# A bias table with fewer copies, PSUM reads moved between engines, and input sums formed in place, in a decoder layer

## The chip, the cores and the metric

The kernel runs on one core of a Trainium2 chip. The metric is the time of one execution on the device in microseconds (us). Engines are named as the profile names them: PE is TensorE's matmul stream, PEld its weight loads, DVE is VectorE, ACT is ScalarE, POOL is GpSimd and SP is SyncE, whose queue (SPq) issues every DMA of this kernel.

## The reference, cut to what matters

One decoder layer on 512 tokens of width 1024 in float32: a SwiGLU feed-forward (FFN) of width 2816, two token mixers side by side (sparse attention with a relative bias, and a gated linear recurrence), their merge, a second such FFN, and a gated per-layer embedding. The two parts that the change touches:

```python
def swiglu(x, w_gate, w_up, w_down):
    return (jax.nn.silu(x @ w_gate) * (x @ w_up)) @ w_down

dist = jnp.maximum(t_pos[None, :, None] - idx, 0)
bias = jnp.moveaxis(rel_bias[rel_bucket(dist)], -1, 2)          # 32 buckets, 8 heads
logits = (jnp.einsum('bqhc,bqkc->bqhk', ql, c_sel) * ATT_SCALE + bias)
```

## The kernel before, in words

**Matmuls.** Every float32 product is three passes: weights and inputs are split into a high part (`hi`, ScalarE copy) and a low part (`lo`, VectorE subtract), and the passes are hi x hi, lo x hi and hi x lo. All of them are issued by one helper, so nearly every row of PE has line L248. A 128x1024 piece of weights arrives in a `raw` tile (5 buffers), and its hi and lo go into a `w` tile (6 buffers of 2112 elements per partition, of which 2048 are used, from an offset `shift`: 0 for plain weights, `SHIFT` for paired ones).

**An FFN** works on 22 column tiles of gate and up in four groups of 6, 4, 6 and 6 tiles. After each group its part of the down product is added to `y`. In the first group four tiles are computed plainly (512 tokens at a time) and two as a pair; all other tiles go in pairs, so an FFN has 1 + 2 + 3 + 3 = 9 pairs.

**A pair** (`pair`, L492) computes two gate tiles (side i = 0) and two up tiles (side i = 1) by Strassen-Winograd's seven half-size products in place of eight. A side needs four sums of weight halves: S1 (POOL, L513), S2 (DVE, L514), S3 (POOL, L517) and S4 (DVE, L520), in place in `raw` or in a sum tile `s` (2 buffers), each then split by ACT (L489) and DVE (L490). The seven products run in the order of `SEVEN`; each is 12 matmuls of 256 columns for each side, so a pair has 7 x 2 x 12 = 168 matmuls. Bank a takes the products number 0, 2, 4 and 6 on top of one another and is read after each: product 6 can't begin on a side before the bank was read for number 4, where C22 = a + P5 is formed (L542, DVE, out of PSUM). POOL then scales side 0's half by R (L551).

**The input sums** (`input_sums`, L459) make T1 to T4 from halves of the scaled input `h`, for all pairs of an FFN, in four steps (k = 0 to 3), each with two scaled copies (`b1`, `b2`: ACT, L467), four POOL subtractions (L471) and four splits (L195, L196). Results of the subtractions go into an `s` tile of the pair's own two buffers. One step is taken before the plain tiles that come next, one after each of them, and what is left ahead of the first pair. `b1`, `b2` and all temporaries of the plain tiles (`hidden`, L372: three each) and of the pairs (four each) are `t` tiles, of which there are 6.

**The bias table** (`bias_vector`, L143) is made at the end of FFN 1's first group: a small matmul and one DVE instruction give `bv` (8 heads on 8 partitions, 384 values each), and one DMA (L157) writes it to DRAM as `bias_d`, 128 copies for each head. Attention later reads it back once for each head (L701) as a 128x256 tile `tp`, in which partition p holds the vector from element 127 - p on: in `bias_d` that is one access pattern, with a step of 383 elements from a partition to the next, which moves to the next copy and one element back.

**Order of the work.** The order on each engine is chosen when the program is built, by a scheduler that follows the order of the code and its own estimate of times; each engine, and the SP queue, then takes its instructions strictly in that order. An instruction that waits holds up all that stand behind it on its engine.

Of the kernel before, what the change touches and what calls it, by code (L numbers as in the profile page):

```python
# [7 lines left out]
F32 = mybir.dt.float32  # L8
# [3 lines left out]
OP = mybir.AluOpType  # L12
PSUM = bass.MemoryType.PSUM

P = 128
# [11 lines left out]
SEVEN = (("a", True, "A11", "B11"), ("b", True, "A12", "B21"), ("a", False, "S2", "T2"), ("c", True, "S1", "T1"),  # L27
         ("a", False, "S3", "T3"), ("c", False, "S4", "B22"), ("a", False, "A22", "T4"))

SHIFT = 16  # L30
FULL = slice(0, NT)
HALF = (slice(0, 256), slice(256, NT))
G_OFF = {n: 8 * i for i, n in enumerate(
# [5 lines left out]
HEADS = 8  # L39
# [11 lines left out]
LEVELS = (1, 2, 4, 8, 16)  # L51
NEAR = 256
BVEC = 384
LEAD = 1
BANKS = {"mm": 2, "pl": 2, "hg": 2, "pt": 1, "po": 1}

# [22 lines left out]
class Layer:  # L79
    def __init__(self, ctx, tc, a, out):  # L80
        self.tc, self.nc, self.a, self.out = tc, tc.nc, a, out

        def pool(name, **kw):
            return ctx.enter_context(tc.tile_pool(name=name, bufs=1, **kw))

        self.const = pool("const")
        self.keep = pool("keep")
        self.wpool = pool("wpool")
        self.tmp = pool("tmp")
        self.psum = pool("psum", space=PSUM)  # L90
        self.dram = pool("dram", space=bass.MemoryType.DRAM)
        self.h_d = self.dram.tile([KT, P, NT], F32, name="h_d")
        self.gate_d = self.dram.tile([2 * KT, P, NT], F32, name="gate_d")
        self.proj_d = self.dram.tile([4, P, D], F32, name="proj_d")
        self.bias_d = self.dram.tile([HEADS, P, BVEC], F32, name="bias_d")
        self.ahead = []
        self.mixing = False
        self.first = {k: iter(v) for k, v in FIRST.items()}
        self.ring = itertools.cycle(("mm", "pl", "mm", "pl", "pt", "po"))
        self.held = None  # L100
        self.lo_engine = self.nc.vector
        self.consts()
# [40 lines left out]
    def bias_vector(self):  # L143


        nc, c = self.nc, self.const
        onehot = self.t(BVEC)[:32]
        nc.sync.dma_start(onehot, self.a["onehot"])
        rel = c.tile([32, HEADS], F32, name="rel")
        nc.sync.dma_start(rel, self.a["rel_bias"])  # L150
        far = c.tile([HEADS, 1], F32, name="far")
        nc.sync.dma_start(far, self.a["rel_far"])
        ps = self.bank("pl")
        nc.tensor.matmul(ps[:HEADS, :BVEC], rel, onehot, start=True, stop=True)
        bv = self.t(BVEC)[:HEADS]
        nc.vector.tensor_scalar(bv, ps[:HEADS, :BVEC], far, 1.0 / ATT_SCALE, op0=OP.subtract, op1=OP.mult)
        nc.sync.dma_start(self.bias_d, bv.unsqueeze(1).to_broadcast([HEADS, P, BVEC]))  # L157

    def gain(self, n):
        return self.vecs[:, G_OFF[n]:G_OFF[n] + KT]  # L160
# [220 lines left out]
    def ffn(self, name, nxt, y, pool, spill=None, begin=None):  # L381
        nc, a = self.nc, self.a
        wg, wu, wd = (a[f"{name}_w_{s}"] for s in ("gate", "up", "down"))
        post = self.ghalf[f"{name}_post"]
        hid_hi = pool.tile([P, INNER, NT], F32R, name="hid_hi")
        hid_lo = pool.tile([P, INNER, NT], F32R, name="hid_lo")
        acc = self.accum(NT)
        for f0, nf, plain in GROUPS:
            first, last = f0 == 0, f0 + nf == FT
            j0 = 0  # L390
            if first and not begin:
                j0 = 2
                w = [self.first_weights(name, (wg[j], wu[j]), D) for j in range(j0)]
                for cols, tags in zip(HALF, (("mm", "mm", "pl", "pl"), ("pt", "po", "mm", "mm"))):
                    ps = [[self.bank(t)[:, :256] for t in tags[2 * j:2 * j + 2]] for j in range(j0)]
                    self.mm3s([(ps[j][i], w[j][i]) for j in range(j0) for i in range(2)], self.hg_hi, self.hg_lo, KT, cols)
                    for j in range(j0):
                        self.hidden(hid_hi, hid_lo, j, *ps[j], cols)
            elif first:
                j0 = 1  # L400
                w = begin[0](wg[0], wu[0])
                ps = self.bank("pl"), self.bank("pt")
                self.mm3s(list(zip(ps, w)), self.hg_hi, self.hg_lo, KT, FULL)
                begin[1]()
                self.hidden(hid_hi, hid_lo, 0, *ps, FULL)
            if first:
                sums = self.input_sums(f"{name}_pre", pool)
                next(sums)
            for j in range(j0, plain):
                pg, pu = self.bank(), self.bank()  # L410
                self.mm3(pg, self.weight(wg[f0 + j], D), self.hg_hi, self.hg_lo, KT, FULL)
                self.mm3(pu, self.weight(wu[f0 + j], D), self.hg_hi, self.hg_lo, KT, FULL)
                self.hidden(hid_hi, hid_lo, j, pg, pu, FULL)
                next(sums, None)
            if first:
                for _ in sums:
                    pass
            for j in range(plain, nf, 2):
                self.pair(pool, [src[f0 + j:f0 + j + 2] for src in (wg, wu)], hid_hi, hid_lo, j)
            w = {}  # L420

            def parts(m, ps, cols, ks):
                if m not in w:
                    w[m] = self.weight(wd[m][:, f0 * P:(f0 + nf) * P], nf * P)
                for k in ks:
                    self.mm3_step(k, ps, w[m], hid_hi, hid_lo, nf, cols)

            def store(m, ps, cols):
                if first:
                    nc.scalar.copy(y[:, m, cols], ps)  # L430
                else:
                    nc.vector.tensor_tensor(y[:, m, cols], y[:, m, cols], ps, op=OP.add)
                if last:
                    self.square_sum(acc[:, cols], y[:, m, cols], m == 0, nc.vector if m == KT - 1 else nc.gpsimd)

            def product(m, cols):
                ps = self.bank()[:, :cols.stop - cols.start]
                parts(m, ps, cols, range(nf))
                store(m, ps, cols)


            early = 3
            ps = [self.bank() for _ in range(early)]
            for ks in (range(nf - 2), range(nf - 2, nf)):
                for m in range(early):
                    parts(m, ps[m], FULL, ks)
            for m in range(early):
                store(m, ps[m], FULL)
            if last:
                self.last_product(product, y, acc, post, nxt, TURN[name], spill, early)  # L450
                if begin:
                    self.ple_proj(pool)
            else:
                for m in range(early, KT):
                    product(m, FULL)
                if first and begin:
                    begin[2]()

    def input_sums(self, gname, pool):  # L459

        nc = self.nc
        self.T = [pool.tile([P, 2, 4, 256], F32R, tag="T", name=f"T{i}", bufs=4) for i in range(4)]
        one, two = HALF
        for k in range(4):
            b1, b2 = self.t(), self.t()
            for b, kk in ((b1, k), (b2, k + 4)):
                nc.scalar.activation(b, self.h[:, kk, :], AF.Copy, scale=self.gain(gname)[:, kk:kk + 1])  # L467
            s = self.sum_tile(pool).rearrange("p (i t) -> p i t", i=4)
            for i, (x, z) in enumerate(((b1[:, two], b1[:, one]), (b2[:, two], s[:, 0]), (b2[:, two], b1[:, two]),
                                        (b2[:, one], s[:, 1]))):  # L470
                nc.gpsimd.tensor_tensor(s[:, i], x, z, op=OP.subtract)  # L471
                self.split(self.T[i][:, 0, k, :], self.T[i][:, 1, k, :], s[:, i])
            yield

    def sum_tile(self, pool):
# [16 lines left out]
    def pair(self, pool, srcs, hid_hi, hid_lo, j):  # L492


        nc = self.nc
        pool_, dve = nc.gpsimd, nc.vector
        low, high = slice(0, 512), slice(512, 1024)
        one, two = HALF
        sides = []
        last = self.weight_tile(SHIFT)  # L500
        for i, src in enumerate(srcs):
            r = [self.raw_tile() for _ in range(2)]
            for x, z in zip(r, src):
                nc.sync.dma_start(x, z)
            w = [self.weight_tile(SHIFT) for _ in range(3)]
            s = self.sum_tile(pool)
            at = {"A11": (w[0], low), "A12": (w[0], high), "S1": (w[1], low), "S2": (w[1], high), "S3": (w[2], low),
                  "A22": (w[2], high), "S4": (last, (low, high)[i])}
# [22 lines left out]
        def after(i, n):  # L531
# [7 lines left out]
            elif n == 3:  # L539
                keep(i, "P5", "c", "acc")  # L540
            elif n == 4:
                dve.tensor_tensor(o2[:, two], b["a"], k["P5"], op=OP.add)  # L542
            elif n == 5:
                dve.tensor_tensor(o1[:, two], b["c"], k["U2"], op=OP.add)
                if i == 0:
# [144 lines left out]
    def attention(self, hd):  # L690


        nc = self.nc
        o, m = hd % 2, hd // 2
        rows = slice(o * IDX, (o + 1) * IDX)
        if o == 0:
# [1 line left out]
        kh = self.kh[o]  # L698
        st = self.stacked(self.qa[m], o, 0)
        tp = self.mixp.tile([P, NEAR], F32, tag="tp", name="tp", bufs=2)  # L700
        nc.sync.dma_start(tp, bass.AP(tensor=self.bias_d.tensor, offset=self.bias_d.offset + hd * P * BVEC + P - 1,  # L701
                                      ap=[[BVEC - 1, P], [1, NEAR]]))
        po = self.bank("po")
        pair = slice(m * P, (m + 1) * P)
        yield
# [550 lines left out]
```

## Time and profile before

| | |
|---|---|
| median of 3 runs | 1279.94 us (1278.24 to 1281.02) |
| profiled execution | 1276.73 us |
| its span, first to last instruction | 1274.9 us |
| busy share PE, DVE, ACT, POOL | 94%, 73%, 51%, 43% |
| mean granted TensorE clock | 0.983 |

The profiled execution stands 3.2 us under the median and 1.8 us over its own span. Times in the rows are counted from the first instruction. A busy share is of the whole span; matmuls overlap, so PE's is an upper bound of its work. In a row of a timeline the bracket gives how long the engine sat idle before the instruction, and which instruction ended that wait.

### The profile page before, as it was taken

The numbers are of one execution on the slowest core, as the hardware profiler recorded it, in microseconds if no ns is written. First come the engines' busy times: TensorE is split into PE (matmuls) and PEld (weight loads), VectorE is DVE, ScalarE is ACT, GpSimd is POOL, SyncE is SP. The second block draws the span as 40 slices with busy tenths as digits, with TensorE's granted clock in tenths as the row PEclk, the third lists the DMA queues.
The fourth block names the chain that finished last, engine by engine and source line by source line (L and its number), as shares of the span: only waits on it lengthen the run. The fifth ranks groups of instructions, "written<-read, shape, count | busy, mean of one in ns | idle before, by whom it ended". The sixth has DMA issues, their size and how long they took to land.

```text
span 1274.9 us, 19983 instructions
## 1 busy us (share of the span) xinstructions
PE 1196.0 (94%) x7532; PEld 1068.4 (84%) x7532; DVE 926.4 (73%) x1532; ACT 644.9 (51%) x1155; POOL 547.8 (43%) x524
## 2 busy tenths in 40 slices
PE   7999299999999999999899999999799999999997
PEld 6888298989999887887688878898689899899976
DVE  7774278976967749999657658477757788678586
ACT  6553143534545546555667655455545444355353
POOL 3532133433446304453747552444433344344474
PEclk9999599999999999999999999999899999999999
DMA  8042332241354412322222226320222323233231
GB/s 277 3 154 58 67 110 98 88 144 67 110 189 158 149 50 67 116 92 80 86 88 92 79 80 219 123 84 29 75 96 71 128 92 124 83 101 117 98 117 66
DMA packets 47897, 131.52 MB, mean 103 GB/s; under 512 B 5400, under 2 KB 10680, under 8 KB 47800
## 3 DMA queue, kind: packets, MB, share of 16 engines
q1 hardware_dynamic: 47800, 130.24, 31.9%
q8 instruction: 59, 0.97, 0.3%
q14 instruction: 38, 0.31, 0.1%
HBM read 118.16 MB, written 12.06 MB: 102 GB/s over the span
## 4 chain that ended last, share of the span: by engine, by line
PE 55%; DVE 25%; issue 8%; ACT 5%; POOL 4%; DMA 3%; SPq 0%; DVEq 0%; POOLq 0%; ACTq 0%
PE mm L248 21%; PE pl L248 15%; PE pt L248 6%; PE po L248 6%; DVE w L490 5%; DVE w L174 2%; DVE hg_lo L293 2%; DVE sc L687 2%; DVE h L347 2%; DVE z L345 1%; DVE small L686 1%; DMA g<-gate_d 1%; PE po L736 1%; DVE s L514 1%; DMA raw<-ffn_w_gate 1%
## 5 line engine op out<-in xcount | busy, mean ns | idle before, releaser
L248 PE MATMUL mm<-hg_hi,w 128*128 128x512 f32 (+1 forms) x984 | 268.1, 355 | 3.4 <-ACT hg_hi L195 1.5
L248 PEld LDWEIGHTS mm<-hg_hi,w 128*128 128x128 f32 x984 | 170.9, 189 | 27.3 <-ACT hg_hi L195 1.7
L172 ACT ACTIVATE w<-raw 128x1024 fp32r<-128x1024 f32 (+5 forms) x149 | 135.1, 913 | 87.2 <-PE mm L248 24.4
L174 DVE TENSOR_TENSOR w<-raw,w 128x1024 fp32r<-128x1024 f32 (+5 forms) x133 | 146.9, 1112 | 38.2 <-ACT w L172 37.7
L248 PE MATMUL mm<-hg_lo,w 128*128 128x512 f32 (+1 forms) x492 | 172.9, 353 | 1.3 <-DVE hg_lo L293 1.3
L490 DVE TENSOR_TENSOR w<-raw,w 128x1024 fp32r<-128x1024 f32 (+1 forms) x108 | 146.1, 1368 | 19.3 <-ACT w L489 19.3
L513 POOL TENSOR_TENSOR s<-raw 128x512 f32<-128x512 f32 x36 | 52.5, 1459 | 220.2 <-DMA raw<-ffn_w_gate 110.2
L248 PE MATMUL pl<-hg_hi,w 128*128 128x256 f32 (+1 forms) x504 | 111.7, 314 | 27.6 <-ACT acc L529 22.5
L489 ACT ACTIVATE w<-raw 128x1024 fp32r<-128x1024 f32 (+1 forms) x108 | 95.6, 912 | 61.1 <-DMA raw<-ffn_w_up 26.1
L248 PEld LDWEIGHTS pl<-hg_hi,w 128*128 128x128 f32 x504 | 82.8, 193 | 32.9 <-ACT acc L529 22.7
L248 PEld LDWEIGHTS mm<-hg_lo,w 128*128 128x128 f32 x492 | 92.2, 188 | 13.2 <-DVE hg_lo L293 1.5
L286 POOL TENSOR_TENSOR acc<-acc,sq 128x256 f32<-128x256 f32 x78 | 67.5, 870 | 58.9 <-ACT sq L285 54.8
L248 PE MATMUL mm<-T,w 128*128 128x256 f32 x552 | 74.2, 284 | 7.7 <-DVE t L542 4.3
L248 PE MATMUL pl<-hid_hi,w 128*128 128x512 f32 (+1 forms) x276 | 78.2, 367 | 0.0
L248 PE MATMUL pl<-hg_lo,w 128*128 128x256 f32 (+1 forms) x252 | 77.6, 311 | 0.7 <-DVE hg_lo L293 0.7
L514 DVE TENSOR_TENSOR s<-s,raw 128x512 f32<-128x512 f32 x36 | 32.3, 896 | 63.1 <-POOL s L513 63.1
L248 PEld LDWEIGHTS mm<-T,w 128*128 128x128 f32 x552 | 68.8, 192 | 9.2 <-DVE t L542 5.1
L489 ACT ACTIVATE w<-s 128x1024 fp32r<-128x1024 f32 x36 | 38.2, 1062 | 75.3 <-DVE s L514 23.7
L248 PE MATMUL pl<-T,w 128*128 128x256 f32 x540 | 72.3, 283 | 3.9 <-ACT w L489 2.0
L248 PE MATMUL mm<-hid_hi,w 128*128 128x512 f32 (+1 forms) x264 | 73.9, 365 | 0.0
L248 PEld LDWEIGHTS pl<-T,w 128*128 128x128 f32 x540 | 67.4, 192 | 4.9 <-ACT w L489 2.2
L578 POOL TENSOR_TENSOR t<-t,R 128x512 f32<-128x512 f32 x36 | 59.2, 1647 | 25.9 <-ACT t L577 25.8
(358 smaller groups left out, 3026.5 us busy)
## 6 DMA issues: line engine op xcount, KB each, us to landing
raw<-ffn_w_gate SPq DMA_DIRECT2D x43, 512.0 KB, 4.0
raw<-ffn_w_up SPq DMA_DIRECT2D x43, 512.0 KB, 3.6
raw<-ffn_w_down SPq DMA_DIRECT2D x48, 384.0 KB, 3.8
raw<-w_gates SPq DMA_DIRECT2D x16, 512.0 KB, 3.5
raw<-ffn_w_down SPq DMA_DIRECT2D x16, 256.0 KB, 2.7
gate_d<-t SPq DMA_DIRECT2D x16, 256.0 KB, 2.0
raw<-w_br SPq DMA_DIRECT2D x8, 512.0 KB, 3.5
raw<-w_out SPq DMA_DIRECT2D x8, 512.0 KB, 3.9
```

What stands on the lines that cost most here:

```text
L172: hi = nc.scalar.activation(w[:, 0, c], raw[:, c], AF.Copy)
L174: lo = eng.tensor_tensor(w[:, 1, c], raw[:, c], w[:, 0, c].bitcast(F32), op=OP.subtract)
L248: i = self.nc.tensor.matmul(*args, **kw)
L286: eng.tensor_tensor(acc[:, c:c + 256], acc[:, c:c + 256], sq, op=OP.add)
L293: lo = nc.vector.scalar_tensor_tensor(self.hg_lo[:, k, cols], self.h[:, k, cols], g, self.hg_hi[:, k, cols].bitcast(F32), op0=OP.mult, op1 ...
L347: eng.tensor_tensor(self.h[:, k, c], self.h[:, k, c], z, op=OP.add)
L489: self.nc.scalar.activation(w[:, 0], raw, AF.Copy)
L490: eng.tensor_tensor(w[:, 1], raw, w[:, 0].bitcast(F32), op=OP.subtract)
L513: pool_.tensor_tensor(s[:, low], r[1][:, low], r[1][:, high], op=OP.add)
L514: dve.tensor_tensor(s[:, high], s[:, low], r[0][:, low], op=OP.subtract)
L578: nc.gpsimd.tensor_tensor(z, z, self.R, op=OP.mult)
L687: nc.vector.match_replace(sc, best, sc, TAKEN)
```

## The change

There are five edits:

- `bias_d` holds 23 copies for each head in place of 128. The read for attention steps by (376, 16 times) and (383, 8 times): partition 8a + b reads copy a + b from element 127 - 8a - b on, which are the same values as before.
- C22: ACT copies the PSUM bank into `o2`, then POOL adds P5 to it in SBUF. One DVE instruction less and one more on ACT and on POOL, for each side of each pair.
- The input sums go into a `t` tile and, for T3 and T4, into halves of `b1` and `b2` themselves, not into an `s` tile.
- Two steps of the input sums, not one, are taken before the plain tiles.
- The offset of paired weights in their `w` tile goes in turn through 16, 8, 20 and 12 elements from pair to pair, where it was always 16.

```diff
-SHIFT = 16
+SHIFT = (16, 8, 20, 12)
+STEP = 8
+COPIES = P // STEP + STEP - 1
...
-        self.bias_d = self.dram.tile([HEADS, P, BVEC], F32, name="bias_d")
+        self.bias_d = self.dram.tile([HEADS, COPIES, BVEC], F32, name="bias_d")
+        self.shift = itertools.cycle(SHIFT)
...
-        nc.sync.dma_start(self.bias_d, bv.unsqueeze(1).to_broadcast([HEADS, P, BVEC]))
+        nc.sync.dma_start(self.bias_d, bv.unsqueeze(1).to_broadcast([HEADS, COPIES, BVEC]))
...
                 sums = self.input_sums(f"{name}_pre", pool)
                 next(sums)
+                next(sums)
...
-            s = self.sum_tile(pool).rearrange("p (i t) -> p i t", i=4)
-            for i, (x, z) in enumerate(((b1[:, two], b1[:, one]), (b2[:, two], s[:, 0]), (b2[:, two], b1[:, two]),
-                                        (b2[:, one], s[:, 1]))):
-                nc.gpsimd.tensor_tensor(s[:, i], x, z, op=OP.subtract)
-                self.split(self.T[i][:, 0, k, :], self.T[i][:, 1, k, :], s[:, i])
+            s = self.t()
+            for i, (o, x, z) in enumerate(((s[:, one], b1[:, two], b1[:, one]), (s[:, two], b2[:, two], s[:, one]),
+                                           (b1[:, two], b2[:, two], b1[:, two]), (b2[:, one], b2[:, one], s[:, two]))):
+                nc.gpsimd.tensor_tensor(o, x, z, op=OP.subtract)
+                self.split(self.T[i][:, 0, k, :], self.T[i][:, 1, k, :], o)
...
-        last = self.weight_tile(SHIFT)
+        shift = next(self.shift)
+        last = self.weight_tile(shift)
...
-            w = [self.weight_tile(SHIFT) for _ in range(3)]
+            w = [self.weight_tile(shift) for _ in range(3)]
...
             elif n == 4:
-                dve.tensor_tensor(o2[:, two], b["a"], k["P5"], op=OP.add)
+                nc.scalar.copy(o2[:, two], b["a"])
+                pool_.tensor_tensor(o2[:, two], o2[:, two], k["P5"], op=OP.add)
...
-        nc.sync.dma_start(tp, bass.AP(tensor=self.bias_d.tensor, offset=self.bias_d.offset + hd * P * BVEC + P - 1,
-                                      ap=[[BVEC - 1, P], [1, NEAR]]))
+        nc.sync.dma_start(tp, bass.AP(tensor=self.bias_d.tensor, offset=self.bias_d.offset + hd * COPIES * BVEC + P - 1,
+                                      ap=[[BVEC - STEP, P // STEP], [BVEC - 1, STEP], [1, NEAR]]))
```

## Rows read from the trace of the kernel before

**Rows 1.** The page: granted TensorE clock in 40 slices, in tenths
```profile
PEclk9999599999999999999999999999899999999999
```

**Rows 2.** Waits of PE: for which instruction, us in total, times, longest
```profile
PE pl L248 <- ACT acc L529: 22.5, 1, 22.5
...
PE mm L248 <- DVE t L542: 4.3, 4, 2.1
...
PE pl L248 <- DVE t L542: 1.0, 1, 1.0
```

**Rows 3.** Timeline around the bias table's DMA: SP queue, ACT, PE (start, duration)
```profile
114.30 0.79 SPq L157 DMA_DIRECT2D bias_d<-t  x1
115.76 14.31 SPq L504 DMA_DIRECT2D raw<-ffn_w_up  x2
...
149.93 1.06 ACT L489 ACTIVATE w<-raw 128x1024 fp32r<-128x1024 f32 x1 [26.15 <-DMA raw<-ffn_w_up]
...
151.29 0.80 PE L248 MATMUL pl<-hg_hi,w 128*128 128x256 f32 x2 [22.49 <-ACT acc L529]
...
155.78 2.93 PE L248 MATMUL pt<-T,w 128*128 128x256 f32 x12 [1.56 <-DVE t L542]
```

**Rows 4.** DMA issues: times, KB each, median us to landing
```profile
raw<-ffn_w_up SPq DMA_DIRECT2D x43, 512.0 KB, 3.6
...
bias_d<-t SPq DMA_DIRECT2D x1, 1536.0 KB
...
tp<-bias_d SPq DMA_DIRECT2D x8, 128.0 KB, 3.1
```

**Rows 5.** Stretches: length, busy of PE, PEld, DVE, ACT, POOL, PEclk, DMA, GB/s
```profile
138.00:146.00 8.00, 0.00 (x0) 0.00 (x0) 0.00 (x0) 0.00 (x0) 0.00 (x0) 0.50 0.45 49
56.00:80.30 24.30, 20.73 (x171) 19.88 (x170) 20.46 (x28) 12.53 (x23) 8.34 (x8) 1.00 0.33 115
113.56:179.41 65.85, 41.81 (x337) 41.32 (x337) 28.90 (x40) 19.40 (x34) 15.99 (x11) 0.79 0.40 78
897.72:928.29 30.57, 22.26 (x170) 21.76 (x168) 23.97 (x33) 14.99 (x28) 12.95 (x12) 0.83 0.28 91
960.95:1000.53 39.58, 39.58 (x338) 39.57 (x336) 28.74 (x39) 20.13 (x35) 15.92 (x11) 1.00 0.30 94
1043.00:1066.00 23.00, 20.59 (x173) 20.19 (x172) 22.73 (x25) 11.08 (x18) 13.42 (x9) 1.00 0.28 87
```

**Rows 6.** Timeline of FFN 2's first pair: POOL and PE
```profile
904.68 1.71 POOL L513 TENSOR_TENSOR s<-raw 128x512 f32<-128x512 f32 x1 [3.30 <-DVE T L196]
...
909.30 0.58 PE L248 MATMUL po<-T,w 128*128 128x256 f32 x1 [5.76 <-ACT w L489]
...
912.64 0.58 PE L248 MATMUL mm<-T,w 128*128 128x256 f32 x1 [2.55 <-ACT w L489]
```

**Rows 7.** Timeline of FFN 1's first pair: POOL and PE
```profile
63.13 1.29 POOL L513 TENSOR_TENSOR s<-raw 128x512 f32<-128x512 f32 x1 [4.21 <-DVE w L490]
...
67.88 0.39 PE L248 MATMUL pl<-T,w 128*128 128x256 f32 x1 [2.01 <-ACT w L489]
```

**Rows 8.** Single lines: engine, operation, count, ns min/median/max
```profile
L542 DVE TENSOR_TENSOR t<-mm,acc x12: 409/416/425, 73.6 to 1157.8; 128x256 f32<-128x256 f32 x12
...
L529 ACT COPY z<-mm x12: 350/364/376, 70.4 to 1147.1; 128x256 f32<-128x256 f32 x12
...
L551 POOL TENSOR_TENSOR t<-t,R x18: 736/1645/1652, 74.1 to 1173.5; 128x256 f32<-128x256 f32 x18
...
L490 DVE TENSOR_TENSOR w<-s,w x36: 1206/1224/2201, 61.8 to 1158.8; 128x1024 fp32r<-128x1024 f32 x36
```

**Rows 9.** Chain of waits: runs of 256-column matmuls (start, us, count)
```profile
160.53 1.36 PE mm L248 x12
...
339.01 1.41 PE pt L248 x12
...
824.44 2.88 PE mm L248 x24
```

## The prediction

> **What bounds the kernel now.** PE does. I read the clock row of the page first, then PE's waits, then the stretches of the waits that count, then the timelines inside them. The clock row [rows 1] has one slice at half speed, the fifth (127 to 159 us), so PE stood still there. PE's waits [rows 2] show why little else matters: one wait of 22.5 us for ACT's L529, then small ones. The first pairs of the two FFNs wait for ACT's L489 [rows 6, 7], and there are four rows of waits for DVE's L542, of which the first and the last stand, 10.5 us in ten waits. So the sum goes by these places; elsewhere PE already runs without a break.
>
> **The 22.5 us and the bias table.** The timeline [rows 3] has the chain. SPq issues the table's write at 114.30 and the next pair's up weights at 115.76. ACT then sits 26.15 us in front of L489 until those weights land at 149.9; the L529 behind it, a copy that frees a PSUM bank, comes too late, and PE restarts at 151.29, at half clock (0.50 at 138 to 146 us [rows 5]). In that stretch only the table moves, at 49 GB/s. Its 1536 KB [rows 4] are 1.573 MB: 32 us at that rate, which reaches from 115.8 to 148. Weights of 512 KB land 3.6 us after their issue in the median [rows 4].
>
> With 23 copies the table is 23/128 of that, 283 KB: 5.8 us, so it is out at about 121.6. Weights that start only then land at 125.2; L489 and the copy take 1.06 and 0.36 us [rows 3, 8], which is 126.6. PE came to its wait at 151.29 - 22.49 = 128.8. That is 2 us to spare; each us beyond it would be paid by PE. What it is worth: FFN 1's second group took 65.85 us, FFN 2's, the same two pairs without a table, 39.58 with PE busy all through [rows 5]; the difference is 26.3. By its own matmul speed (28 runs of 12 at 1.36 [rows 9], 38.1) it is 27.8. The half clock and the 1.56 us for L542 [rows 3] are inside. I take 27; at worst, with 3 us left of the wait, 24. The read back keeps its size: eight loads of 128 KB, 3.1 us each [rows 4], issued ahead of a tile that attention uses later; PE's waits name none of them, so I cost the new access pattern at nothing, and at up to 3.1 us for each of the eight were that cover gone.
>
> **The input sums.** FFN 2's first pair takes 30.57 us, FFN 1's 24.30 [rows 5]; 14 runs of 12 at 1.36 us are 19.0. So 11.5 and 5.3 us are lost. In FFN 2 POOL's first sum of weight halves, L513, starts at 904.68 after a wait for DVE's split of T [rows 6]: nothing in its arithmetic needs T, but its `s` tile was still held by the input sums. The sums S1 and S2 follow, and PE waits 5.76 and 2.55 us for their L489; the remaining 3.2 us are mostly the half clock that the stop brings. In FFN 1 the second L513 waits 4.21 us for an L490, again for an `s` tile, and PE pays 2.01 us and smaller waits [rows 7]. With the input sums out of `s`, L513 needs only its weights, which were there, and POOL's turn. Then the T tiles are next to be late: the last step still stands behind the last plain tile, though the third now stands one tile earlier. So I leave a quarter: 9 of 11.5 and 4.3 of 5.3. The bounds are 3 and 1 (T becomes the wait) and the whole.
>
> What the edit charges: three `t` tiles a step in place of two, held until DVE has split T3 and T4. Two steps fill all six, so the first plain tile behind them must wait with its PSUM reads until the first step is through: four POOL instructions of 0.74 us or more (L551's least, the same shape [rows 8]) and their splits, 3 to 5 us. DVE would stand in that wait with the weight splits behind it. It is covered by the banks of the next plain tiles and by weights split ahead; uncovered it is 3 to 5 us in each FFN, and that is inside the lower bounds just given.
>
> **C22 over ACT.** Each of 18 pairs loses two DVE instructions of 0.416 us and gains two ACT copies of 0.36 us and two POOL adds of 0.74 to 1.65 us [rows 8]: DVE -15 us, ACT +13, POOL +27 to +59. What is on the path is the bank. PE's product 6 waits for L542, which stands in DVE's queue behind splits of 1.2 us; 10.5 less the 1.56 inside the table's stretch is 8.95. ACT is busy 11 of 23 us where DVE is busy 22.7 (the last of [rows 5]), so the copy comes at once unless it lands behind an L489 of 1.06 us. Behind the copy on ACT stand the next L489s, which have time. Side 0's add feeds L551, which sat waiting for L542 anyway; nothing of PE waits for either before the down product. I take 7, bounds 2 and 8.95.
>
> The trace also has a price for the adds: L551, of this shape, takes 0.736 us at least and 1.645 in the median, and L490 1.2 in the median and 2.2 at most [rows 8], so POOL and DVE hold each other up. The Trainium skill says it as a rule (SBUF — State Buffer, section Who interferes with whom): a VectorE instruction with two SBUF inputs and a GpSimd instruction that reads SBUF exclude each other for a whole instruction. By that rule L542, with one input in PSUM, held up nobody, and its successor on POOL does; by the rule alone the edit would give back what L542 costs, and more where DVE is full. I go by the rows: a delay of DVE reaches PE only through a weight split that is late, and PE's waits hardly name one.
>
> **The offsets.** Paired matmuls run at 1.36 or 1.41 us a dozen, plain 256-column ones, at offset 0, at 2.88 for two dozen [rows 9]: 113, 118 and 120 ns each. Of the 18 pairs 7 run mostly at the first and 11 at the second, all at offset 16, so offset alone doesn't decide. No row has 8, 20 or 12. Bounds: all pairs at the first, 11 x 14 x 0.05 = 7.7 us less; all at the third, 7 x 14 x 0.08 + 11 x 14 x 0.03 = 12.5 us more. I take nothing, since one state of each kind lies on either side of the mean.
>
> **The sum.** 27 + 9 + 4.3 + 7 = 47.3 us. The profiled execution of 1276.7 us would be 1229.4; the runs' median stands 3.2 above it, so 1279.9 - 47.3 = **1233 us**.
>
> **The rivals.**
> - *Only the table pays.* T, not `s`, holds the first pairs, and DVE or ACT takes L542's place. For: DVE is full in the second pairs (22.7 of 23.0 us [rows 5]) and the last step of the sums still stands behind the last plain tile. Against: PE's waits name L489 and L542, not T. 27 plus some 3: 1250 us.
> - *The offsets cost.* All pairs at the plain matmuls' speed: 47.3 - 12.5, 1245 us. For: offset 0 does run slower. Against: no row with these offsets.
> - *The table doesn't shrink in time*, because its time isn't by the byte: then 20 us remain, 1260. Against: 49 GB/s is level for 8 us with nothing else in motion [rows 5].
> - *Slower: POOL's adds hold up DVE's splits of weights.* Place: the 36 adds. Price: up to 1.65 us each, 59 us, and the 7 of C22 gone: -47.3 + 7 + 59 = 19 us more, 1299 us. It decides once more than (47.3 - 7)/36 = 1.1 us of each add reaches PE. For: L490's 2.2 us. Against: DVE is freed of 15 us by the same edit, and groups' first and last pairs leave it idle a quarter of the time (28.7 of 39.6 us [rows 5]).
>
> **How the numbers follow.** The forecast 0.65, only the table 0.17, the offsets 0.09, the table unshrunk 0.04, the slower one 0.05. All best ends add to 27.8 + 11.5 + 5.3 + 8.95 + 7.7 = 61 (1219 us); 24 + 3 + 1 + 2 - 12.5 = 17.5 (1262) are all worst. The range takes the forecast with its terms' bounds, the offsets case and half of the case with the table alone: 1221 to 1251. About 0.2% (2.6 us) can be told from no change. All cases but the last are faster by more: 0.95. Of the last, 0.01 ends level and 0.04 slower.
>
> **What would show it.** In the profile after, ACT's 26 us wait for weights near 115 is gone or under 10, the fifth slice of the clock row is full, and FFN 1's second group takes 38 to 42 us. L513 of the first pairs no longer waits for L196 or L490, and these pairs take 19 to 23 us. PE's waits on L542's bank fall from 10.5 to under 3 us, with ACT as their releaser. Runs of 12 paired matmuls stay between 1.36 and 1.44 us. I am wrong if PE waits at the second group for weights still, if waits for T or for L490 take the place of those for L489, or if DVE's L490 grows by more than its idle time in the pairs.

## The result, and the profile after

| | before | after |
|---|---|---|
| median | 1280.48 us (1278.24 to 1281.28) | 1238.01 us (1237.39 to 1240.75) |
| profiled execution, span | 1276.7, 1274.9 us | 1238.0, 1236.3 us |
| mean granted clock | 0.983 | 0.997 |

The change makes the kernel faster: the ratio of after to before is 0.9675, 95% interval 0.9656 to 0.9694. I had said 1233 us, 1221 to 1251. Lines shift: before's L157, L248, L489, L490, L513, L529 are L161, L252, L494, L495, L519, L535 after. ACT's copy of C22 is L548, POOL's add L549.

Two rows of the page after, busy time of the engines and granted clock in 40 slices (before, DVE was busy for 926.4 us, ACT for 644.9, POOL for 547.8):

```profile
PE 1193.5 (97%) x7532; PEld 1067.1 (86%) x7532; DVE 918.5 (74%) x1496; ACT 657.1 (53%) x1191; POOL 590.9 (48%) x560
...
PEclk9999999999999999999999999999999999999999
```

The half-speed fifth slice of [rows 1] is full. The stretches of the first pairs and of the two-pair groups after, in order of time (columns as in [rows 5]):

```profile
56.19:76.61 20.42, 19.81 (x169) 19.41 (x168) 15.78 (x25) 12.86 (x25) 7.30 (x8) 1.00 0.44 138
110.11:150.05 39.94, 39.94 (x337) 39.94 (x337) 28.27 (x36) 20.91 (x38) 19.50 (x15) 1.00 0.36 98
870.75:894.14 23.39, 23.33 (x182) 22.37 (x181) 17.79 (x28) 15.19 (x32) 13.29 (x13) 1.00 0.39 119
923.87:963.68 39.81, 39.81 (x337) 39.81 (x336) 27.59 (x35) 21.63 (x39) 20.06 (x15) 1.00 0.30 94
```

Against [rows 5], the first pair of FFN 1 went from 24.30 to 20.42 us, its second group from 65.85 to 39.94, the first pair of FFN 2 from 30.57 to 23.39. The last holds 13 matmuls of the down product that had stood behind it (that part fell from 32.66 to 29.73 us, 2.9 less), so like with like it is 20.5. In the 39.94 PE has no idle time left.

The timeline after around the table's DMA, SP queue and ACT:

```profile
110.85 0.80 SPq L161 DMA_DIRECT2D bias_d<-t  x1
112.31 4.73 SPq L510 DMA_DIRECT2D raw<-ffn_w_up  x2
114.73 1.16 ACT L494 ACTIVATE w<-raw 128x512 fp32r<-128x512 f32 x2 [1.10 <-PE mm L252]
...
120.62 1.07 ACT L494 ACTIVATE w<-raw 128x1024 fp32r<-128x1024 f32 x1
```

Where ACT sat for 26.15 us in [rows 3], it now waits 1.10 us, and for PE. The table's 184 packets of 1536 bytes run in the trace from 112.28 to 118.20: 5.9 us, 48 GB/s, as before.

The span fell by 38.6 us: 25.9 in FFN 1's second group, 3.9 and 10.1 in the two first pairs, and 2.5 in all other groups together, which makes 42.4. Of that 3.3 us were given back between FFN 1's last pair and FFN 2's first (539.1 to 542.4) and 0.5 ahead of FFN 1's second group. PE's waits after that belong to these places:

```profile
PE pt L252 <- DVE hg_lo L297: 3.9, 4, 2.7
...
PE pl L252 <- ACT sq L535: 2.2, 2, 1.6
...
PE mm L252 <- ACT sq L535: 1.8, 1, 1.8
...
PE po L252 <- ACT sq L535: 1.0, 1, 1.0
...
PE pl L252 <- DVE t L551: 0.7, 1, 0.7
```

The ten waits for L542 [rows 2] are gone. In their place stand waits for ACT's keep of P1 (L535), and one wait has grown: before, PE's waits for `hg_lo` on the bank `pt` were 1.8 us, the longest 0.8. Its place is the start of FFN 2, where the timeline after shows POOL, DVE and PE so:

```profile
835.02 1.46 POOL L519 TENSOR_TENSOR s<-raw 128x512 f32<-128x512 f32 x1
835.26 2.37 DVE L351 TENSOR_TENSOR h<-h,z 128x256 f32<-128x256 f32 x2
...
837.32 1.44 POOL L523 TENSOR_TENSOR raw<-raw 128x512 f32<-128x512 f32 x1
837.55 2.75 DVE L297 SCALAR_TENSOR_TENSOR hg_lo<-h,vecs,hg_hi 128x256 fp32r<-128x256 f32 x3
...
839.09 0.58 PE L252 MATMUL pt<-hg_lo,w 128*128 128x256 f32 x1 [2.72 <-DVE hg_lo L297]
```

The freed L519 and L523, sums for a pair that starts at 870, now run among the norm's work ahead of FFN 2, and DVE's instructions beside them take 2.37 us for two and 2.75 for three. Behind PE's wait of 2.72 us the granted clock is 0.59 on the mean from 839 to 843 us, so for most of these 4 us it is at the lower of its two levels. The 3.3 us given back are thus 1.9 us more of waiting and, for the rest, this slow stretch.

### The profile page after: what moved, and what is told of

Same layout as the page of the kernel before. It is cut to its first block, busy times and chain, and to the rows that moved or that the text cites. A ratio compares the mean times of both kernels' runs of the same rounds, so it can differ in the third digit from the quotient of the medians.

```text
span 1236.3 us, 20073 instructions
## 1 busy us (share of the span) xinstructions
PE 1193.5 (97%) x7532; PEld 1067.1 (86%) x7532; DVE 918.5 (74%) x1496; ACT 657.1 (53%) x1191; POOL 590.9 (48%) x560
## 4 chain that ended last, share of the span: by engine, by line
PE 56%; DVE 22%; POOL 7%; issue 7%; ACT 5%; DMA 3%; SPq 0%; DVEq 0%; POOLq 0%; ACTq 0%
PE mm L252 22%; PE pl L252 15%; PE po L252 6%; PE pt L252 6%; DVE w L495 3%; DVE w L178 3%; DVE hg_lo L297 2%; DVE sc L694 2%; DVE h L351 2%; DVE small L693 1%; DMA g<-gate_d 1%; POOL t L549 1%; PE po L743 1%; DVE z L349 1%; POOL raw L523 1%
## 5 line engine op out<-in xcount | busy, mean ns | idle before, releaser
L252 PE MATMUL mm<-hg_hi,w 128*128 128x512 f32 (+1 forms) x984 | 268.8, 356 | 3.3 <-ACT hg_hi L199 1.5
L252 PEld LDWEIGHTS mm<-hg_hi,w 128*128 128x128 f32 x984 | 171.2, 189 | 27.4 <-ACT hg_hi L199 1.7
L252 PE MATMUL mm<-hg_lo,w 128*128 128x512 f32 (+1 forms) x492 | 173.1, 354 | 1.2 <-DVE hg_lo L297 1.2
L176 ACT ACTIVATE w<-raw 128x1024 fp32r<-128x1024 f32 (+5 forms) x149 | 135.3, 914 | 72.1 <-PE mm L252 20.5
L495 DVE TENSOR_TENSOR w<-raw,w 128x1024 fp32r<-128x1024 f32 (+1 forms) x108 | 146.2, 1367 | 16.4 <-ACT w L494 16.2
L519 POOL TENSOR_TENSOR s<-raw 128x512 f32<-128x512 f32 x36 | 51.7, 1436 | 197.8 <-DMA raw<-ffn_w_gate 110.4
L252 PE MATMUL pl<-hg_hi,w 128*128 128x256 f32 (+1 forms) x504 | 110.5, 312 | 6.5 <-ACT w L176 5.1
L494 ACT ACTIVATE w<-raw 128x1024 fp32r<-128x1024 f32 (+1 forms) x108 | 96.0, 914 | 36.7 <-PE mm L252 11.0
L252 PEld LDWEIGHTS mm<-hg_lo,w 128*128 128x128 f32 x492 | 92.2, 188 | 13.1 <-DVE hg_lo L297 1.4
L252 PEld LDWEIGHTS pl<-hg_hi,w 128*128 128x128 f32 x504 | 81.7, 190 | 12.9 <-ACT w L176 5.1
L252 PE MATMUL pl<-hid_hi,w 128*128 128x512 f32 (+1 forms) x276 | 78.4, 367 | 0.0
L252 PE MATMUL pl<-hg_lo,w 128*128 128x256 f32 (+1 forms) x252 | 77.1, 309 | 0.7 <-DVE hg_lo L297 0.7
L252 PE MATMUL mm<-T,w 128*128 128x256 f32 x552 | 73.6, 282 | 2.3 <-ACT sq L535 1.8
L252 PE MATMUL pl<-T,w 128*128 128x256 f32 x540 | 72.8, 284 | 2.3 <-ACT sq L535 2.2
L549 POOL TENSOR_TENSOR t<-t,acc 128x256 f32<-128x256 f32 x36 | 45.4, 1260 | 59.7 <-ACT t L548 59.6
L252 PE MATMUL mm<-hid_hi,w 128*128 128x512 f32 (+1 forms) x264 | 73.9, 365 | 0.0
L252 PEld LDWEIGHTS mm<-T,w 128*128 128x128 f32 x552 | 68.7, 190 | 3.0 <-ACT sq L535 2.2
L252 PEld LDWEIGHTS pl<-T,w 128*128 128x128 f32 x540 | 68.0, 192 | 2.9 <-ACT sq L535 2.6
L495 DVE TENSOR_TENSOR w<-s,w 128x1024 fp32r<-128x1024 f32 x36 | 57.9, 1607 | 12.8 <-ACT w L494 12.8
```

Source lines behind the costliest of these rows:

```text
L176: hi = nc.scalar.activation(w[:, 0, c], raw[:, c], AF.Copy)
L252: i = self.nc.tensor.matmul(*args, **kw)
L494: self.nc.scalar.activation(w[:, 0], raw, AF.Copy)
L495: eng.tensor_tensor(w[:, 1], raw, w[:, 0].bitcast(F32), op=OP.subtract)
L519: pool_.tensor_tensor(s[:, low], r[1][:, low], r[1][:, high], op=OP.add)
L549: pool_.tensor_tensor(o2[:, two], o2[:, two], k["P5"], op=OP.add)
```

## The experiments

**Each edit alone.** Four kernels, each the kernel before with one part of the change: the table; C22; the input sums in place with two steps; the offsets. Their diffs are those parts of the change.

> The kernel before with the table of 23 copies and its read alone. Theory (the whole price is the wait behind the table's DMA and the half clock after it): FFN 1's second group goes from 65.9 to about 39 us, nothing else moves, 26 us less in all (about 1254 us). Rival (a good part of the 26 us in the changed kernel came from the copy of C22 and from the offsets, since the group also had a wait for L542): under 23 us, with PE still waiting in that group.

> The kernel before with C22 read by ACT alone. Theory (the bank is what counts, and ACT gives a part of it back, since in the changed kernel PE waits 5 us for L529's copies that stand behind weight splits on ACT): the ten waits for L542 go, new ones of 4 to 6 us for ACT come, 3 to 6 us less in all. Rival 1 (ACT's waits only arise with the other edits): 9 us less. Rival 2 (POOL's adds hold up DVE by as much as was gained): within 2 us of before or slower.

> The kernel before with the input sums in place and two steps ahead, and nothing else. Theory: FFN 1's first pair falls from 24.3 to about 20.5 us and FFN 2's from 30.6 to about 23.5, and at FFN 2's start PE pays some 3 us because POOL's first sum of weight halves now runs among the residual and prenorm work and holds up DVE there; 7 to 8 us less in all. Rival (the loss at FFN 2's start belongs to another edit): 11 us less, and no wait over 1 us for hg_lo at FFN 2's start.

> The kernel before with paired weights at offsets 16, 8, 20, 12 in turn, and nothing else. Theory (the offsets other than 16 hold paired matmuls at about 118.4 ns, whatever came before, and only offset 16 can run at 113.3): more pairs at 118.4 than before, 2 to 5 us slower. Rival 1 (the state is set by whether PE enters the pair out of a wait, not by the offset): the same pairs at 113.3 as in the kernel before, no change within 1 us. Rival 2 (offsets shorten the time): over 1 us faster.

| part alone | median, us | ratio to before | 95% interval | us |
|---|---|---|---|---|
| table | 1256.25 | 0.9815 | 0.978 to 0.985 | -23.7 |
| C22 | 1274.28 | 0.9954 | 0.9938 to 0.9971 | -5.9 |
| input sums, two steps | 1269.09 | 0.9916 | 0.9893 to 0.9939 | -10.8 |
| offsets | 1284.22 | 1.0029 | 1.0014 to 1.0044 | +3.7 |

The us column is the ratio less one, times the 1280.6 us of the kernel before beside them. The table's theory said 26 us, its rival under 23; the interval, 19 to 28 us less, holds both. The group decides: it took 40.57 us in place of 65.85, 25.3 less, and the only wait of PE left in it is 1.0 us for C22, so the rival's part is small. In the other groups of this profile PE's waits for C22 are longer, 13.2 us in all against 10.5. With C22 alone the waits for L542 are gone, and 6.0 us of waits for ACT's keep of P1 stand in their place, as its theory said. The sums gave 10.8 us by the ratio (7.8 to 13.7) and 7.4 by the profiled executions, so the totals don't tell the theory's 7 to 8 from the rival's 11; the places are the theory's: FFN 2's first pair 23.0 us, and PE's longest wait for `hg_lo` 2.7 us. The offsets cost what their theory said. The parts add to -36.7 us, the whole is -41.6 by its ratio. The intervals of the parts are too wide to say whether the 5 us between them are real.

**The offsets, taken back in the whole.**

```diff
-SHIFT = (16, 8, 20, 12)
+SHIFT = 16
```

> The changed kernel with one edit taken back: paired weights always at offset 16. Theory (the offsets cost, because only pairs at 16 can run a dozen matmuls in 1.36 us and one pair in four has that offset): 3 to 5 us faster than the changed kernel, so 1233 to 1235 us, with more than three pairs whose matmuls run at 113 ns. Rival (the 3.7 us of the offsets alone were a chance of the order of work and go with the other edits): within 1 us of the changed kernel, 1237 to 1239.

1236.39 us, ratio 0.9650 (0.9629 to 0.9671): 3.2 us less than the change by the ratios and 1.6 by the medians, at the theory's lower edge or under it, and the two intervals overlap; that the offsets cost time rests on the kernel with the offsets alone. The mechanism is plainer in the rows. Timeline, runs of 12 paired matmuls in FFN 1's second group, first after (this pair at offset 8), then with offset 16 always:

```profile
118.74 1.58 PE L252 MATMUL mm<-T,w 128*128 128x256 f32 x12
120.15 1.59 PE L252 MATMUL pl<-T,w 128*128 128x256 f32 x12
121.58 1.58 PE L252 MATMUL pt<-T,w 128*128 128x256 f32 x12
```

```profile
115.23 1.52 PE L250 MATMUL pt<-T,w 128*128 128x256 f32 x12
116.59 1.52 PE L250 MATMUL po<-T,w 128*128 128x256 f32 x12
117.95 1.52 PE L250 MATMUL mm<-T,w 128*128 128x256 f32 x12
```

From start to start that is 1.42 and 1.36 us, and this stretch took 38.2 us with offset 16, the best end of the prediction's working.

**One step of the input sums, not two, in the whole.** Its edit is the second `next(sums)` taken out.

> The changed kernel with one edit taken back: one step of the input sums ahead of the plain tiles, not two. Theory (freeing the s tiles is what pays, and the second early step only moves T forward): FFN 2's first pair within 1.5 us of the 23.4 of the changed kernel, and the 2.7 us wait of PE for hg_lo at FFN 2's start stays, since it comes from POOL's first weight sums, which no longer wait for an s tile; in all within 2 us of the changed kernel. Rival (T is the next to be late, so the second step carries the gain): both first pairs longer by 2 us or more each and the kernel 4 us or more slower.

1243.23 us, ratio 0.9693 (0.9672 to 0.9713): 5 us over the change by the medians, 2.3 by the ratios, whose intervals overlap. Both theories were half wrong. FFN 1's first pair is unchanged (20.2 us). FFN 2's takes 30.4, of which 6.1 are down matmuls that moved in, so 24.3 against 20.5: there T is late. That is still 6.3 us under the 30.57 of before, which the freed `s` tiles give without the second step. PE's waits in this kernel, and the stretch behind the first of them at a granted clock of 0.79:

```profile
PE pl L251 <- DVE T L199: 1.3, 1, 1.3
...
PE po L251 <- DVE T L199: 0.8, 1, 0.8
```

```profile
884.00:892.00 8.00, 6.16 (x27) 5.30 (x28) 6.44 (x12) 2.92 (x8) 3.75 (x4) 0.79 0.49 145
```

The wait of 2.7 us for `hg_lo` stayed, so it does not come from the second step. Two more slices below full clock, in the mixers, make the rest of this kernel's profile longer; why is open.

**C22 taken back in the whole.**

```diff
-                nc.scalar.copy(o2[:, two], b["a"])
-                pool_.tensor_tensor(o2[:, two], o2[:, two], k["P5"], op=OP.add)
+                dve.tensor_tensor(o2[:, two], b["a"], k["P5"], op=OP.add)
```

> The changed kernel with one edit taken back: C22 formed by VectorE out of PSUM again. Theory (the waits for L542 return, 10 to 13 us of them, and those for ACT's copy and keeps, some 6 us, go): 4 to 7 us slower than the changed kernel, 1242 to 1245 us. Rival (POOL's adds cost as much as the copy gives, by exclusion of VectorE and GpSimd): within 1.5 us of it. Second rival (with the other edits in place the waits for L542 cost more than they did alone): 8 us slower or more.

1246.44 us, ratio 0.9721 (0.9701 to 0.9742): 5.9 us slower than the change by the ratios. PE's waits for ACT's keep of P1 fell to 0.6 us, and those for C22 came back on the four banks (L547 is this kernel's C22), 9.7 us:

```profile
PE mm L251 <- DVE t L547: 4.4, 4, 2.3
...
PE po L251 <- DVE t L547: 2.5, 3, 1.4
...
PE pl L251 <- DVE t L547: 1.5, 2, 0.9
...
PE pt L251 <- DVE t L547: 1.3, 2, 1.0
```

**A table of 64 copies, in the whole.** `COPIES = 64`; the rest as in the change.

> The changed kernel with 64 copies for each head in the table's write, not 23 (the read is as with 23). Theory (the table blocks the weights behind it for its bytes at 49 GB/s): 786 KB take 16 us, the weights behind land 10 us later than with 23 copies; PE had some 2 us to spare with 23, so it waits about 8 us in FFN 1's second group, which then takes 47 to 51 us in place of 39.9 with a half-clock stretch after the wait; 8 to 11 us slower than the changed kernel. Rival (the time goes by something other than the bytes, or PE had much more to spare): under 3 us slower.

1247.63 us, ratio 0.9738 (0.9719 to 0.9756): 8.1 us slower by the ratios, FFN 1's second group 50.66 us. Timeline, ACT and PE; then the stretch around the restart:

```profile
131.33 1.06 ACT L493 ACTIVATE w<-raw 128x1024 fp32r<-128x1024 f32 x1 [10.96 <-DMA raw<-ffn_w_up]
...
132.70 0.80 PE L251 MATMUL pl<-hg_hi,w 128*128 128x256 f32 x2 [7.07 <-ACT acc L534]
```

```profile
131.00:136.00 5.00, 3.30 (x15) 3.30 (x16) 2.12 (x2) 3.09 (x6) 3.35 (x3) 0.50 0.04 14
```

It is the chain of [rows 3], shorter: ACT waits for the weights, PE for ACT, then half clock. PE waited 7.1 us where 8 were foreseen, so 23 copies leave some 3 us to spare, not 2, by this estimate. The table's time goes by its bytes: in the traces its packets run for 5.9 us with 23 copies, 16.3 with 64 and 32.5 with 128, each time at 48 GB/s.

**FFN 2's first sums behind the norm, and offset 16 always.**

```diff
-            eng.tensor_tensor(acc[:, c:c + 256], acc[:, c:c + 256], sq, op=OP.add)
+            self.last_sq = eng.tensor_tensor(acc[:, c:c + 256], acc[:, c:c + 256], sq, op=OP.add)
...
-            pool_.tensor_tensor(s[:, low], r[1][:, low], r[1][:, high], op=OP.add)
+            first = pool_.tensor_tensor(s[:, low], r[1][:, low], r[1][:, high], op=OP.add)
+            if hold:
+                self.issue_after(first, hold)
```

`hold` is `self.last_sq`, the norm's last square sum, and is handed over in FFN 2's first pair alone. The lines that do so, and those of the offset, are left out here.

> The changed kernel with offset 16 always, and with GpSimd's first sum of weight halves in FFN 2's first pair ordered behind its last square sum of the norm ahead of FFN 2. Theory (freed of their s tiles, these sums slipped between the norm's work, and VectorE's residual adds and splits of the input, two SBUF inputs each, were held up by them): the wait of PE for hg_lo falls from 2.7 us to 0.8 or less, FFN 2's first pair stays at 23 to 24 us, and the kernel is 2 to 3.5 us faster than the one with offset 16 always, so about 1233 us. Rival (the wait comes from the norm's own order): the wait stays at 2.7 us, and the time within 1 us of that kernel.

1234.68 us, ratio 0.9639 (0.9615 to 0.9663), the fastest here. Its DVE and POOL at the same place (L349 and L295 are the residual add and the low part of the input), and PE's wait:

```profile
831.92 1.29 DVE L349 TENSOR_TENSOR h<-h,z 128x256 f32<-128x256 f32 x2
833.13 0.87 DVE L295 SCALAR_TENSOR_TENSOR hg_lo<-h,vecs,hg_hi 128x256 fp32r<-128x256 f32 x2
834.16 0.73 DVE L295 SCALAR_TENSOR_TENSOR hg_lo<-h,vecs,hg_hi 128x256 fp32r<-128x256 f32 x1 [0.16 <-ACT hg_hi L294]
```

```profile
835.54 1.29 POOL L517 TENSOR_TENSOR s<-raw 128x512 f32<-128x512 f32 x1
836.91 1.36 POOL L523 TENSOR_TENSOR raw<-raw 128x512 f32<-128x512 f32 x1
```

```profile
PE pt L250 <- DVE hg_lo L295: 1.8, 4, 0.8
```

The two adds take 1.29 us in place of 2.37, the three splits 1.60 in place of 2.75, and the wait is back at its value before. The granted clock stays at 1.00 there (833.6 to 837 us). Up to FFN 2's first pair this profile is 3.9 us shorter than with offset 16 alone; the pair and the down product behind it take 54.2 us against 52.9, with two waits of PE for T of 0.4 us each, so 2.6 us remain. The pair itself took 21.5 us, not the 23 to 24 foreseen, because no down matmuls moved into it. The total fell by 1.4 us by the ratios, under the 2 to 3.5 foreseen, and these intervals can't tell it from nothing; the wait and the place are shown.

**P5 added by DVE in SBUF, in the whole.**

```diff
-                pool_.tensor_tensor(o2[:, two], o2[:, two], k["P5"], op=OP.add)
+                dve.tensor_tensor(o2[:, two], o2[:, two], k["P5"], op=OP.add)
```

> The changed kernel, but P5 is added in SBUF by VectorE, not by GpSimd; ScalarE still copies the bank. Theory (what pays is that the bank is freed by an engine with time to spare, and GpSimd's adds cost PE little): within 1.5 us of the changed kernel, or slower by up to 3 us since VectorE has its 36 instructions back. Rival (GpSimd's adds hold up VectorE's splits, and that is what is missing from the gain of C22): 2 us faster or more.

1243.77 us, ratio 0.9709 (0.9684 to 0.9733): 5 us slower than the change beside it by the medians, 4 by the ratios. That is on the other side from the rival; whether it is beyond the theory's 3, these intervals, which overlap, don't decide. The page's busy times, DVE's row of the add (L548), and PE's waits on ACT's keeps:

```profile
PE 1196.9 (96%) x7532; PEld 1070.4 (86%) x7532; DVE 912.3 (73%) x1532; ACT 656.5 (53%) x1191; POOL 549.2 (44%) x524
```

```profile
L548 DVE TENSOR_TENSOR t<-t,acc 128x256 f32<-128x256 f32 x36 | 15.1, 444 | 6.3 <-ACT t L547 6.2
```

```profile
PE mm L251 <- ACT sq L534: 4.1, 4, 2.6
...
PE pl L251 <- ACT sq L534: 3.8, 3, 2.8
```

DVE does 36 instructions of 15.1 us more than after and is yet busy 6 us less (912.3 against 918.5). Against this kernel, then, POOL's adds held up DVE by some 21 us in all, 0.6 for each. But DVE's place for the add changes the order of the rest. Against the kernels with C22 out of PSUM the adds cost DVE less: with the 15 us of those 36 instructions taken off, DVE is busy 911 us before and 917.7 with C22 alone, and 911 with C22 taken back against 918.5 after. So the cost is 6 to 21 us, 0.2 to 0.6 for each. Being rid of it did not help PE here. On DVE the add stands behind splits of 1.2 to 2.3 us, POOL's scaling and ACT's silu wait for it (3.36 and 6.52 us ahead of PE's wait of 2.6), and the keep of P1 stands behind the silu on ACT.

**Four other offsets.** `SHIFT = (0, 32, 48, 64)`; the rest as in the change.

> The changed kernel with the offsets 0, 32, 48 and 64 elements in turn in place of 16, 8, 20 and 12. Theory (a paired matmul runs in 113 ns where the offset is an odd multiple of 16 elements, so 48 like 16, and in 118 to 120 elsewhere): of the four only pairs at 48 show runs of twelve at 1.36 us. First rival (any offset but 0 that is a multiple of 16 elements will do): 32, 48 and 64 show them. Second rival (offset 16 is not special, the state comes from what the pair waited for): no offset shows more of them than the others.

1240.24 us, ratio 0.9682 (0.9644 to 0.972), no different from the change. No pair shows runs at 1.36 us. So the theory and its first rival fall. The second rival's sign is there, but its premise is not: offset 16 shows such runs in the other kernels. The pitch is the time from the start of one matmul to the start of the next. Its mean for the paired matmuls, pair by pair, from the traces (intervals under 130 ns):

| offset, elements | 0, 64 | 32 | 20 | 8, 12 | 48 | 16 |
|---|---|---|---|---|---|---|
| ns for one matmul | 119.8 to 120.0 | 118.6 to 119.9 | 118.6 to 118.8 | 118.2 to 118.4 | 117.5 to 117.8 | 113.3 or 117.8 |

Runs of twelve in this kernel's FFN 1, start to start 1.41 us at offset 48, then 1.44 at 64:

```profile
136.19 1.57 PE L251 MATMUL mm<-T,w 128*128 128x256 f32 x12
137.60 1.57 PE L251 MATMUL pl<-T,w 128*128 128x256 f32 x12
...
180.76 1.60 PE L251 MATMUL mm<-T,w 128*128 128x256 f32 x12
182.20 1.60 PE L251 MATMUL pl<-T,w 128*128 128x256 f32 x12
```

**The change once more, beside these three.**

> The changed kernel itself, beside the three others on one chip, so that differences of 2 to 3 us among them can be read: 1236 to 1241 us, and a ratio to the kernel before of 0.966 to 0.969.

1238.74 us, ratio 0.9677 (0.965 to 0.9704), as expected.

## Why the prediction was right, point by point

**The table: right, 27 said, 25.9 measured.** The 5.8 us of the write were 5.9, the second group fell into the 38 to 42 us named, and ACT's wait, PE's stop and the half clock went together. With 64 copies the same arithmetic gave 8 us of waiting and the trace 7.1. The missing 1.1 us, and more, are the offsets': with offset 16 the stretch takes 38.2 us, 27.6 less than before, which is the 27.8 named as the best end.

**The input sums: mechanism right, 13.3 said, 14.0 gained and 3.3 given back.** FFN 1's pair gave 3.9 for 4.3, FFN 2's 10.1 for 9 (its 23.39 us lie just outside the 19 to 23 I named, the 20.5 like with like inside). The quarter left for T was not needed with two steps; with one, T holds FFN 2's pair, as the text feared, at 3.9 us. The step that failed is the sentence that freed sums need "only its weights, which were there, and POOL's turn": POOL's turn came too early, and what the two sums hold up there costs PE 3.3 us, half clock included. I had looked for the charge in the plain tile behind the two steps, where PE pays nothing. The late-sums kernel shows the cause: the same sums a few us later, and the wait is back at 0.8 us, with no half clock behind it. The other profiles agree: from FFN 1's last paired matmul to FFN 2's first it is 538.1 to 540.0 us in the four kernels with the sums in `s`, 538.2 with the late sums, and 541.8 to 546.8 in all others, though the mixers in between add a spread of their own.

**C22: right in place, 7 said, 5.9 alone and 5.9 when taken back.** PE no longer waits for C22's read (L548) at all, but where it had waited 10.5 us for L542 it now waits 6.2 for other reads of the banks, 5.5 of them for ACT's keeps and 0.7 for L551 (after, DVE's sum with U2), not under 3 as I wrote. I had L489 in front of the copy; it is the next pair's keep of P1 that is late. Timeline after, POOL, ACT and PE at the hand-over to the third pair of a group:

```profile
213.31 1.72 POOL L549 TENSOR_TENSOR t<-t,acc 128x256 f32<-128x256 f32 x1
215.00 1.29 POOL L583 TENSOR_TENSOR t<-t,R 128x512 f32<-128x512 f32 x1
```

```profile
216.31 0.64 ACT L584 ACTIVATE t<-t 128x512 f32<-128x512 f32 x1 [5.71 <-POOL t L583]
216.86 1.99 ACT L494 ACTIVATE w<-raw 128x1024 fp32r<-128x1024 f32 x2
...
218.75 0.62 ACT L584 ACTIVATE t<-t 128x512 f32<-128x512 f32 x1
219.27 0.35 ACT L535 COPY sq<-mm 128x256 f32<-128x256 f32 x1
```

```profile
219.68 1.80 PE L252 MATMUL mm<-T,w 128*128 128x256 f32 x12 [1.76 <-ACT sq L535]
```

ACT idles 5.71 us in front of a silu that waits for POOL, then does two splits and another silu before the 0.35 us that PE waits for. POOL's add itself has a small part in this: the scaling L583 starts as the add ends, and its input from DVE's L551 was ready at 214.8, about 0.2 us earlier.

**POOL's adds against DVE: the rival is wrong, its mechanism is there.** An add took POOL 1.26 us on the mean (45.4 us for 36, inside the 27 to 59 named). The slower rival needed 1.1 us of each add on PE; each cost DVE 0.2 to 0.6, C22 over ACT gained 5.9 us with them, and the kernel with the adds on DVE is slower. What PE pays where POOL holds up DVE depends on what DVE has in hand: at FFN 2's start it is the input of the next matmuls, and there two residual adds take 2.37 us in place of 1.29. The Trainium skill (SBUF — State Buffer, section Who interferes with whom) says that a VectorE instruction with two SBUF inputs contends with a GpSimd instruction that reads SBUF. The trace agrees in that place.

**The offsets: wrong, 0 said, about 3.5 lost.** The bounds held it (7.7 to the good, 12.5 to the bad), and my point value rested on nothing but the middle. Only offset 16 has runs at 1.36 us, so 13 of the 18 pairs lost that chance.

**The sum.** 47.3 said against 42 by the medians and 38.6 by the profiled executions. The 8.7 us between 47.3 and 38.6 are 1.1 in the table's group, 3.3 at FFN 2's start, 0.5 ahead of the second group and 4.5 in the other groups, where 7 was said for C22 and 2.5 came; 0.7 more than said came in the first pairs. The offsets' loss is inside the first and the fourth of these. That the medians stand 4 us nearer is in part luck: the profiled execution of before was 3.2 us under its median.

## What to carry to other kernels

A buffer freed for one engine moves that engine's next work forward as far as the order allows: look at what runs there, and tie the work behind it by an order of issue if it is not needed yet. A slow DMA is worth its bytes at its own rate, here 48 GB/s at three sizes, and the work that waits for the transfers behind it inherits that; look whether copies that only serve an access pattern can be cut. Work taken off a full engine is worth what waited behind it in that engine's queue, not its busy time: 15 us off DVE gave 5.9 here.

## What the runs showed of the hardware that I had not expected

- The pitch of the paired 256-column matmuls depends on where their weights start in their tile, in steps from 113.3 to 120.0 ns, and at offset 16 it has two states, 113.3 and 117.8 ns, one after the other in the same pair. 48 has the slower of these almost throughout. What sets the state is open.
- The bias table's write, from 8 partitions, ran at 48 GB/s with 23 copies as with 128 (49), while in the 3 us after it the core's DMA moved 323 GB/s. In the write of 128 copies the DMA engines were busy for 0.45 of their time [rows 5]. Whether the few partitions, the packets of 1536 bytes or the repeated source make it slow, no run here tells.
- DVE's residual adds and splits took up to 1.8 times as long beside two POOL sums of 1.4 us (2.37 against 1.29 us, 2.75 against 1.60).
